# Taking the feed-forward part's low operand halves off GpSimd and onto VectorE, with VectorE's step reordered

## The chip, the core and the metric

One core of one Trainium2 chip runs the whole kernel in one launch. The metric is device time in microseconds (us), the median over several runs. Engines are named as the profile names them: PE (TensorE's matmuls), PEld (its weight loads), DVE (VectorE), ACT (ScalarE), POOL (GpSimd), SP (SyncE, which here issues DMAs).

## What is computed

One encoder layer over 2048 tokens of width 1024. The change lies in its last part, the feed-forward block:

```
x = x + (gelu(gate) * val) @ w_down,   [gate | val] = dwconv3(rmsnorm(x) @ w_up),   D_FF = 2816
out = rmsnorm(x)
```

`w_up` is 1024 x 5632, `w_down` 2816 x 1024, the convolution is depthwise over three neighbouring tokens, everything is float32. Attention, the recurrent group and the output projection come before and are not touched.

## The kernel before, in words

**Split operands.** Each float32 matrix operand is split in two: a high part (`hi`, the operand rounded to fp32r) and a low part (`lo` = operand minus `hi`). A product is three matmuls, hi by hi, hi by lo and lo by hi. ACT makes the high part with a copy, and another engine makes the low part with one subtraction (`tensor_tensor`, subtract), which needs the high part. In the feed-forward block POOL makes the low parts of the weights and of some activations, DVE the others.

**Class `Up`** computes rmsnorm(x) @ w_up. It runs 44 steps: 22 channel blocks for the first half of the tokens (steps 0 to 21), then the same 22 for the second half (steps 22 to 43). A step multiplies a 2 x 2 block of weights with a 2 x 2 block of activations by seven products instead of eight (`product(s, 0)` to `product(s, 6)`), on sums and differences of the blocks. A product is 12 matmuls of 128 x 128 by 128 x 512, a step 84. Its seven activation operands ("11", "T2", "T3", "21", "T1", "22", "T4" in `ORDER`) live in 15 slots `b0` to `b14` of 128 x 2048 values, and stay for 22 steps. In step 21 they are exchanged (`refill`, `refill_more`): the second half's blocks are fetched from `h2_d` (`fetch`, tile `b..f`), differences formed (`minus`, L773), and each is split again (`high_b`, L789 on ACT; `low_b`, L795).

Each step's weights come by DMA into `wr` (`load_w`, L809); DVE forms four sums (`sums_w`, L817 to L820, tile `sw`); ACT and POOL split four groups g = 0 to 3 into tiles `wg` (`high_w`, L832; `low_w`, L837). Groups 0, 1, 2 have 128 x 1024 values, group 3 has 128 x 512. Group 0 serves products 0 and 3, group 1 products 1 and 2, group 2 products 4 and 5, group 3 product 6.

The products land in eight PSUM banks `q`. DVE (`add`, L876; `c21`, L928) and ACT (copies, L886 and L913) join them to the rows `u` of gate and value. ACT then starts the convolution (`center`, L946: middle tap and bias), DVE adds the outer two taps (`taps`, L954, one `scalar_tensor_tensor` each), ACT applies GeLU (`gelu`, L960), DVE multiplies gate and value (`glu`, L966) and SP stores the result to `a_d`. The value's half of a step's convolution is done in the next step.

**Class `Down`** computes the product with `w_down` in 48 pieces of 48 matmuls or fewer. `load_w` and `load_a` fetch, `split_w` and `split_a` split (both L74 for the high and L77 for the low part; weights in slots `b`, activations in `dah`, `dal`). It begins inside step 43, by `prefetch`.

**Order.** PE, DVE, ACT and POOL run `Up` and `Down` in the order in which the code is written, each engine its own instructions in turn. SP's DMAs, and the few `Up` instructions issued while the output projection runs (`first_weights`), are ordered by the scheduler. An instruction that waits holds up everything behind it on its engine.

## Time and profile before

| | us |
|---|---|
| median of 3 runs (2776.57 to 2779.14) | 2779.02 |
| the profiled execution, its own time | 2781.06 |
| span of that execution in the trace | 2779.3 |
| PE busy in the span | 2649.6 (95%) |
| DVE busy | 1929.2 (69%) |
| ACT busy | 1291.5 (46%) |
| POOL busy | 1090.6 (39%) |

`Up` runs on PE from about 1329 to 2277 us of the span, `Down` from there to the end. The span is 1.8 us shorter than the profiled execution's own time, and that execution is 2.0 us above the median. How to read it: busy PE is not the whole answer, since a matmul at half clock is also busy; so stretches are compared by their length, by what PE waits for in them, and by the granted clock.

### The profile page before, as it was taken

Reading aid. Unit: us, or ns where it says so; the run is one execution under the profiler, and the core shown is the slowest. Engines: PE = TensorE matmul, PEld = TensorE weight load, DVE = VectorE, ACT = ScalarE, POOL = GpSimd, SP = SyncE. Lnnn points to the kernel's source line nnn. Section 1 sums busy time; section 2 is a strip of 40 time slices with the busy share of each in tenths; the row PEclk is TensorE's granted clock in tenths of the full one; section 3 lists DMA queues with packets and bytes.
Section 4 is the critical chain, followed back from the end, with each engine's and each line's share of the span. In section 5 each row is a group of like instructions: output and inputs, shape, how many; then the busy total and the mean of one; then the engine's idle time right before and its main releaser. Section 6 shows DMA issues by size and latency. Waiting matters only on the chain.

```text
span 2779.3 us, 33388 instructions
## 1 busy us (share of the span) xinstructions
PE 2649.6 (95%) x13168; PEld 2147.5 (77%) x13168; DVE 1929.2 (69%) x2055; ACT 1291.5 (46%) x1625; POOL 1090.6 (39%) x628
## 2 busy tenths in 40 slices
PE   7999999899999999999799999879999999999998
PEld 6878778678888887778577777657777778888887
DVE  5453554699999998443699999999999983222333
ACT  4343453588888888322443433343343351122222
POOL 1013322256676767300454554545455553012000
PEclk9999999899999999999899999989999999999999
DMA  5422121401111012334222122312222244344443
GB/s 191 118 84 70 63 85 67 184 18 54 54 54 54 24 31 72 125 125 163 91 84 76 69 83 76 114 61 84 76 81 72 76 168 165 127 154 174 159 159 129
DMA packets 122381, 271.90 MB, mean 98 GB/s; under 512 B 15792, under 2 KB 52144, under 8 KB 115056
## 3 DMA queue, kind: packets, MB, share of 16 engines
q1 hardware_dynamic: 120016, 263.63, 27.7%
q0 software_dynamic: 1632, 4.46, 0.5%
q8 instruction: 103, 1.69, 0.3%
q10 hardware_dynamic: 576, 1.69, 0.2%
q14 instruction: 54, 0.44, 0.1%
HBM read 187.94 MB, written 81.79 MB: 97 GB/s over the span
## 4 chain that ended last, share of the span: by engine, by line
PE 59%; DVE 25%; issue 9%; ACT 4%; POOL 2%; DMA 1%; SPq 0%; DVEq 0%; ACTq 0%; POOLq 0%
DVE acc L954 11%; PE sc L407 7%; PE pd L82 6%; PE pd L80 6%; PE pd L81 6%; PE ps L82 4%; PE ps L81 4%; PE ps L80 4%; PE tp L433 4%; DVE u L876 4%; PE q L864 2%; PE po L82 2%; PE po L81 2%; PE po L80 2%; PE pv L465 2%
## 5 line engine op out<-in xcount | busy, mean ns | idle before, releaser
L954 DVE SCALAR_TENSOR_TENSOR acc<-u,prm,acc 128x1023 f32<-128x1023 f32 (+1 forms) x176 | 474.7, 2697 | 66.9 <-ACT acc L946 63.8
L837 POOL TENSOR_TENSOR wg<-sw,wg 128x1024 fp32r<-128x1024 f32 x88 | 260.8, 2964 | 328.4 <-ACT wg L832 328.4
L77 DVE TENSOR_TENSOR dal<-dal,dah 128x2048 fp32r<-128x2048 f32 (+1 forms) x47 | 111.4, 2374 | 292.7 <-ACT dah L74 292.6
L946 ACT ACTIVATE acc<-u,prm 128x1023 f32<-128x1023 f32 (+1 forms) x88 | 109.3, 1242 | 334.9 <-DVE u L876 196.2
L416 ACT ACTIVATE e<-e,mn 128x2048 f32<-128x2048 f32 x128 | 256.2, 2007 | 15.9 <-DVE mn L411 15.9
L837 POOL TENSOR_TENSOR wg<-wr,wg 128x1024 fp32r<-128x1024 f32 x88 | 204.2, 2321 | 119.0 <-ACT wg L832 119.0
L407 PE MATMUL sc<-ks,qt 64*128 64x512 f32 x1536 | 234.5, 421 | 16.1 <-DVE mn L411 11.9
L74 ACT ACTIVATE dah<-dal 128x2048 fp32r<-128x2048 f32 (+1 forms) x47 | 83.1, 1769 | 309.0 <-DMA dal<-a_d 293.0
L90 POOL TENSOR_TENSOR r<-ss,mhalf 128x1 f32<-128x1 f32 x48 | 27.5, 574 | 482.0 <-DVE ss L88 477.2
L427 DVE SCALAR_TENSOR_TENSOR e<-e,rc,e 128x1024 f32<-128x1024 f32 x128 | 213.9, 1672 | 2.3
L82 PE MATMUL ps<-hT_hi,wl 128*128 128x512 f32 x512 | 199.6, 390 | 0.0
L81 PE MATMUL ps<-hT_lo,wh 128*128 128x512 f32 x512 | 199.6, 390 | 0.0
L80 PE MATMUL ps<-hT_hi,wh 128*128 128x512 f32 x512 | 199.5, 390 | 0.0
L407 PEld LDWEIGHTS sc<-ks,qt 64*128 64x128 f32 x1536 | 147.9, 190 | 62.1 <-DVE mn L411 20.4
L77 POOL TENSOR_TENSOR wTl<-wf,wTh 128x512 fp32r<-128x512 f32 x64 | 127.4, 1991 | 112.4 <-ACT wTh L74 109.8
L411 DVE CUSTOM_DVE_ANT_0 e<-sc,strip,mn 128x1024 f32<-128x1024 f32 x128 | 159.1, 1280 | 16.6 <-PE sc L407 13.8
L876 DVE TENSOR_TENSOR u<-q,u 128x512 f32<-128x512 f32 x220 | 150.6, 685 | 12.8 <-PE q L864 6.9
L77 POOL TENSOR_TENSOR wTl<-wg,wTh 128x1024 fp32r<-128x1024 f32 x64 | 158.1, 2470 | 0.0
L411 DVE CUSTOM_DVE_ANT_0 e<-sc,strip 128x1024 f32<-128x1024 f32 x128 | 150.8, 1212 | 9.0 <-PE sc L407 6.4
L433 PEld LDWEIGHTS tp<-ident,e 128*128 128x128 f32 x1024 | 111.8, 142 | 46.2 <-ACT wTh L74 19.8
L433 PE MATMUL tp<-ident,e 128*128 128x128 f32 x1024 | 142.2, 283 | 0.0
L77 POOL TENSOR_TENSOR wl<-ws,wh 128x1024 fp32r<-128x1024 f32 x16 | 39.1, 2447 | 223.9 <-DVE wh L76 212.0
(348 smaller groups left out, 7122.0 us busy)
## 6 DMA issues: line engine op xcount, KB each, us to landing
wr<-in_w_up_dram SPq DMA_DIRECT2D x88, 512.0 KB, 4.2
dal<-a_d SPq DMA_DIRECT2D x39, 1024.0 KB, 5.0
a_d<-acc SPq DMA_DIRECT2D x66, 256.0 KB, 2.0
xt<-in_x_dram SPq DMA_DIRECT2D x30, 512.0 KB, 4.7
ws<-in_w_qkr_dram SPq DMA_DIRECT2D x16, 512.0 KB, 3.4
qt<-q_d SPq DMA_DIRECT2D x32, 256.0 KB, 3.3
ks<-k_d SPq DMA_DIRECT2D x8, 1024.0 KB, 7.8
vt<-v_d SPq DMA_DIRECT2D x8, 1024.0 KB, 7.1
```

The costliest lines, as they stand in the source:

```text
L77: lo_eng.tensor_tensor(out=lo, in0=src, in1=hi, op=ALU.subtract)
L80: T.matmul(ps, lh, rh, start=first, stop=False)
L81: T.matmul(ps, lh, rl, start=False, stop=False)
L82: T.matmul(ps, ll, rh, start=False, stop=last)
L407: T.matmul(self.sc[c][:, n * CH:(n + 1) * CH], l[rows, q], r[rows, kk], start=i == 0, stop=i == 2)
L411: V.tensor_tensor_reduce(out=self.e[c][:, hf * 1024:(hf + 1) * 1024], in0=self.sc[c], in1=strip[:, off:off + 1024], scale=SLOPES[self.h], ...
L416: A.activation(out=self.e[c], in_=self.e[c], func=AF.Exp, scale=-1.0, bias=self.mn[:, 2 * c + 1:2 * c + 2], accum_out=self.s[c])
L427: V.scalar_tensor_tensor(out=e0, in0=e1, scalar=self.rc, in1=e0, op0=ALU.mult, op1=ALU.add)
L433: T.transpose(tp[:, m, :], self.e[0][:, (4 * i + m) * P:(4 * i + m + 1) * P], ident)
L837: G.tensor_tensor(out=t[:, 1], in0=src, in1=t[:, 0], op=ALU.subtract)
L876: V.tensor_tensor(out=out, in0=a, in1=b_, op=ALU.add)
L954: V.scalar_tensor_tensor(out=acc[:, 0:n], in0=u[:, o + tap:o + tap + n], scalar=prm[:, C_FW + 3 * m + tap:C_FW + 3 * m + tap + 1], in1=acc ...
```

## The change

Every low part of `Up` and `Down` that POOL made is now made on DVE: `low_w` (all weight groups), the splits of "11", "21" and "22", and every `split_w`. After it, POOL is left with one 128 x 1 power per row tile there. Inside `step` some calls move: group 3's low part from the step's start to behind `sums_w`; group 0's to behind `glu`, beside group 1's; group 2's high part to before `center(s, 0)`; and ACT's copy of bank "a" to behind `center(old, 1)` and `gelu(old)`.

```diff
--- before.py
+++ after.py
@@ -834,7 +834,7 @@
 
         def low_w(self, s, g):
             t, src = self.w[s][g]
-            G.tensor_tensor(out=t[:, 1], in0=src, in1=t[:, 0], op=ALU.subtract)
+            V.tensor_tensor(out=t[:, 1], in0=src, in1=t[:, 0], op=ALU.subtract)
 
         def first_weights(self):
             self.load_w(0)
@@ -882,16 +882,16 @@
                 self.c21(old)
             if s > 0:
                 self.high_w(s, 3)
-                self.low_w(s, 3)
-            A.activation(out=ug[:, Y], in_=q("a"), func=AF.Copy)
             if old is not None:
                 self.center(old, 1)
                 self.gelu(old)
+            A.activation(out=ug[:, Y], in_=q("a"), func=AF.Copy)
             if more:
                 self.load_w(s + 1)
                 self.high_w(s + 1, 0)
-                self.low_w(s + 1, 0)
                 self.sums_w(s + 1)
+            if s > 0:
+                self.low_w(s, 3)
             self.product(s, 1)
             hook(1)
             add(uv[:, X], q("d"), ug[:, Y])
@@ -902,9 +902,11 @@
             add(uv[:, X], q("b"), uv[:, X])
             if more:
                 self.high_w(s + 1, 1)
-                self.low_w(s + 1, 1)
             if old is not None:
                 self.glu(old)
+            if more:
+                self.low_w(s + 1, 0)
+                self.low_w(s + 1, 1)
             self.product(s, 3)
             hook(3)
             self.product(s, 4)
@@ -915,9 +917,10 @@
             self.product(s, 5)
             add(ug[:, Y], q("e"), ug[:, Y])
             hook(5)
+            if more:
+                self.high_w(s + 1, 2)
             self.center(s, 0)
             if more:
-                self.high_w(s + 1, 2)
                 self.low_w(s + 1, 2)
             self.taps(s, 0)
             self.product(s, 6)
@@ -999,7 +1002,7 @@
                 raw["21"] = self.fetch(0, 1)
             elif i == 4:
                 raw["T1"] = self.minus(raw["12"], raw["11"])
-                self.split_b("11", G)
+                self.split_b("11", V)
             elif i == 5:
                 raw["T2"] = self.minus(raw["22"], raw["T1"])
                 self.high_b("T2")
@@ -1011,25 +1014,25 @@
                 self.split_b("T3", V)
                 raw["T4"] = self.minus(raw["21"], t2)
                 self.sl.give(t2)
-                self.split_b("21", G)
+                self.split_b("21", V)
 
         def refill_more(self, i):
             if i == 0:
                 self.split_b("T1", V)
-                self.split_b("22", G)
+                self.split_b("22", V)
             elif i == 3:
                 self.split_b("T4", V)
 
         def run(self, down):
             self.low_b("T2", V)
             self.split_b("T3", V)
-            self.split_b("21", G)
+            self.split_b("21", V)
             self.high_w(0, 2)
             self.low_w(0, 2)
             self.split_b("T1", V)
             self.high_w(0, 3)
             self.low_w(0, 3)
-            self.split_b("22", G)
+            self.split_b("22", V)
             self.split_b("T4", V)
             hooks = {NFF - 1: self.refill, NFF: self.refill_more, self.STEPS - 1: lambda i: (self.done_b(i), down.prefetch(i))}
             for s in range(self.STEPS):
@@ -1085,7 +1088,7 @@
             elif i == 2:
                 self.load_w(0, 1)
             elif i == 4:
-                self.split_w(0, 0, G)
+                self.split_w(0, 0, V)
             elif i == 5:
                 self.split_a(0, V)
 
@@ -1120,7 +1123,7 @@
                 nc.sync.dma_start(out[t * P:(t + 1) * P, :], y)
 
             self.load_a(1)
-            self.split_w(0, 1, G)
+            self.split_w(0, 1, V)
             self.split_a(1, V)
             nc.sync.dma_start(g_b, g_fin.partition_broadcast(P))
             last = len(self.order) - NG
@@ -1130,7 +1133,7 @@
                 if i + 2 < len(self.order):
                     self.load_a(i + 2)
                 if c == 0 and n == 0 and g + 2 < NG:
-                    self.split_w(0, g + 2, G)
+                    self.split_w(0, g + 2, V)
                 if i + 2 < len(self.order):
                     self.split_a(i + 2, V)
                 if g == 0:
@@ -1151,7 +1154,7 @@
                 if n == 0 and c == NCH - 1:
                     self.sl.give(*self.w.pop((0, g)))
                     self.load_w(1, g)
-                    self.split_w(1, g, G)
+                    self.split_w(1, g, V)
 
     phase1()
     kp_stack = ExitStack()
```

In the listings below the changed kernel's line numbers are two or three higher from L886 on (L954 of before is L957 there). `u` with a number is a row buffer, `q` with a number a PSUM bank.

**DVE, one step of the second half.** From the last add into the gate row of a step to the middle of the next step: before,

```order
L876 TENSOR_TENSOR u_11979<-q_15558,u_11979 128x512
L954 SCALAR_TENSOR_TENSOR acc<-u_11979,prm,acc 128x1025 x2
L928 TENSOR_TENSOR u_11980<-q_15580,u_11980 128x512
L817 TENSOR_TENSOR sw<-wr 128x512
L818 TENSOR_TENSOR sw<-wr 128x512
L819 TENSOR_TENSOR sw<-sw,wr 128x512
L820 TENSOR_TENSOR sw<-wr,sw 128x512
L876 TENSOR_TENSOR u_11982<-q_15626,u_11981 128x512
L954 SCALAR_TENSOR_TENSOR acc<-u_11980,prm,acc 128x1025 x2
L876 TENSOR_TENSOR u_11982<-q_15642,u_11982 128x512
L966 TENSOR_TENSOR acc<-acc 128x1025
L876 TENSOR_TENSOR u_11981<-q_15626,u_11981 128x512
```

and the same place in the changed kernel up to the new low part of group 3,

```order
L876 TENSOR_TENSOR u_11979<-q_15558,u_11979 128x512
L837 TENSOR_TENSOR wg_15572<-sw,wg_15572 128x1024
L957 SCALAR_TENSOR_TENSOR acc<-u_11979,prm,acc 128x1025 x2
L931 TENSOR_TENSOR u_11980<-q_15580,u_11980 128x512
L817 TENSOR_TENSOR sw<-wr 128x512
L818 TENSOR_TENSOR sw<-wr 128x512
L819 TENSOR_TENSOR sw<-sw,wr 128x512
L820 TENSOR_TENSOR sw<-wr,sw 128x512
L837 TENSOR_TENSOR wg_15607<-wr,wg_15607 128x512
```

A low part of group 2 now stands between the add and the gate's taps, and one of group 3 behind the four sums. The next rows of the changed kernel:

```order
L876 TENSOR_TENSOR u_11982<-q_15625,u_11981 128x512
L957 SCALAR_TENSOR_TENSOR acc<-u_11980,prm,acc 128x1025 x2
L876 TENSOR_TENSOR u_11982<-q_15641,u_11982 128x512
L969 TENSOR_TENSOR acc<-acc 128x1025
L837 TENSOR_TENSOR wg_15617<-wr,wg_15617 128x1024
L837 TENSOR_TENSOR wg_15655<-sw,wg_15655 128x1024
L876 TENSOR_TENSOR u_11981<-q_15625,u_11981 128x512
L876 TENSOR_TENSOR u_11982<-q_15641,u_11981 128x512
L876 TENSOR_TENSOR u_11981<-q_15690,u_11981 128x512
```

Two low parts, of groups 0 and 1, now stand between the product of gate and value and the three adds.

**ACT, the same place.** From the end of one step's products to the GeLU in the next: before,

```order
L940 ACTIVATE u_11979<-halo 128x2
L946 ACTIVATE acc<-u_11979,prm 128x1025
L832 ACTIVATE wg_15047<-sw 128x1024
L832 ACTIVATE wg_15079<-wr 128x512
L886 ACTIVATE u_11981<-q_15065 128x512
L940 ACTIVATE u_11980<-halo 128x2
L946 ACTIVATE acc<-u_11980,prm 128x1025
L960 ACTIVATE acc<-acc 128x1025
```

and in the changed kernel,

```order
L832 ACTIVATE wg_15044<-sw 128x1024
L943 ACTIVATE u_11979<-halo 128x2
L949 ACTIVATE acc<-u_11979,prm 128x1025
L832 ACTIVATE wg_15079<-wr 128x512
L943 ACTIVATE u_11980<-halo 128x2
L949 ACTIVATE acc<-u_11980,prm 128x1025
L963 ACTIVATE acc<-acc 128x1025
L888 ACTIVATE u_11981<-q_15065 128x512
```

The high part of group 2 (`wg<-sw`) moved ahead of `center`, and the copy of bank "a" (`u_11981<-q`) behind the GeLU.

**SP, around the exchange of operands in step 21.** `b8f` is block "11" of the second half, `b2f` is "12", `wr` are weights: before,

```order
L969 DMA a_d_111<-acc 128x511
L809 DMA wr<-in_w_up_dram 128x1024
L986 DMA b8f<-h_d_102 128x4x128
L986 DMA b8f<-h_d_103 128x4x128
L986 DMA b8f<-h_d_104 128x4x128
L986 DMA b8f<-h_d_105 128x4x128
L986 DMA b2f<-h_d_106 128x4x128
L986 DMA b2f<-h_d_107 128x4x128
```

and in the changed kernel,

```order
L972 DMA a_d_111<-acc 128x511
L989 DMA b2f<-h_d_106 128x4x128
L989 DMA b8f<-h_d_102 128x4x128
L989 DMA b8f<-h_d_103 128x4x128
L989 DMA b8f<-h_d_104 128x4x128
L989 DMA b8f<-h_d_105 128x4x128
L989 DMA b2f<-h_d_107 128x4x128
L989 DMA b2f<-h_d_108 128x4x128
```

The half load of `wr` that stood ahead of the eight fetches of "11" and "12" now comes after them (and after those of "21").

## Rows read from the trace of the kernel before

**Rows 1.** The page: busy time of each engine (share of the span, instructions), and the chain that ended last by engine.

```profile
PE 2649.6 (95%) x13168; PEld 2147.5 (77%) x13168; DVE 1929.2 (69%) x2055; ACT 1291.5 (46%) x1625; POOL 1090.6 (39%) x628
...
PE 59%; DVE 25%; issue 9%; ACT 4%; POOL 2%; DMA 1%; SPq 0%; DVEq 0%; ACTq 0%; POOLq 0%
```

**Rows 2.** Busy time by stretch: from:to and length in us, busy us of PE, PEld, DVE, ACT, POOL (instructions), PE's granted clock, DMA share, GB/s. The inner boundaries are the first matmuls of `Up` steps 1, 2, 21, 22, 23 and of `Down`.

```profile
1327.00:1365.93 38.93, 22.89 (x80) 17.75 (x81) 19.78 (x23) 16.38 (x15) 19.68 (x6) 0.74 0.32 107
1365.93:1385.32 19.39, 19.39 (x86) 15.79 (x84) 18.18 (x15) 8.72 (x12) 10.52 (x4) 1.00 0.24 82
1385.32:1772.91 387.59, 372.75 (x1597) 298.55 (x1596) 357.35 (x283) 150.38 (x208) 199.82 (x76) 1.00 0.22 76
1772.91:1793.45 20.54, 19.63 (x85) 15.70 (x84) 18.89 (x16) 9.87 (x12) 11.88 (x5) 1.00 0.61 173
1793.45:1847.84 54.39, 29.89 (x86) 21.56 (x85) 50.32 (x26) 19.55 (x19) 22.98 (x7) 0.69 0.20 67
1847.84:2276.61 428.77, 412.73 (x1765) 329.92 (x1764) 393.34 (x312) 169.83 (x233) 220.25 (x83) 1.00 0.23 81
2276.61:2300.00 23.39, 19.32 (x70) 14.63 (x69) 21.18 (x10) 14.92 (x9) 14.76 (x3) 0.85 0.94 343
2300.00:2779.30 479.30, 470.76 (x2044) 383.20 (x2042) 140.80 (x109) 106.95 (x83) 49.76 (x25) 0.99 0.43 151
```

**Rows 3.** What PE waited for, from 1385.32 to 1772.91 (steps 2 to 20) and from 1847.84 to 2276.61 (steps 23 to 43): us in total, times, longest; in each stretch the only row.

```profile
PE q L864 <- DVE u L876: 14.8, 17, 0.9
...
PE q L864 <- DVE u L876: 16.0, 18, 0.9
```

**Rows 4.** The timeline of DVE in a step of the first half: start, us, engine, line, instruction, count [idle before <- who ended it].

```profile
1600.05 6.50 DVE L954 SCALAR_TENSOR_TENSOR acc<-u,prm,acc 128x1023 f32<-128x1023 f32 x2
...
1608.20 2.20 DVE L876 TENSOR_TENSOR u<-q,u 128x512 f32<-128x512 f32 x3
...
1611.81 4.63 DVE L954 SCALAR_TENSOR_TENSOR acc<-u,prm,acc 128x1023 f32<-128x1023 f32 x2 [1.41 <-ACT acc L946]
...
1616.96 1.18 DVE L817 TENSOR_TENSOR sw<-wr 128x512 f32<-128x512 f32 x1
...
1618.06 0.68 DVE L818 TENSOR_TENSOR sw<-wr 128x512 f32<-128x512 f32 x1
```

**Rows 5.** The timeline of POOL in the same step.

```profile
1599.75 2.38 POOL L837 TENSOR_TENSOR wg<-wr,wg 128x1024 fp32r<-128x1024 f32 x1 [2.70 <-ACT wg L832]
...
1602.09 3.37 POOL L837 TENSOR_TENSOR wg<-sw,wg 128x1024 fp32r<-128x1024 f32 x1
```

**Rows 6.** The timeline of DVE at three places with POOL idle.

```profile
1327.22 2.29 DVE L795 TENSOR_TENSOR b9r<-b5f,b0r 128x2048 fp32r<-128x2048 f32 x1
...
2266.98 2.61 DVE L954 SCALAR_TENSOR_TENSOR acc<-u,prm,acc 128x1025 f32<-128x1025 f32 x2 [0.77 <-ACT acc L946]
...
2285.16 1.23 DVE L966 TENSOR_TENSOR acc<-acc 128x1025 f32<-128x1025 f32 x1
```

**Rows 7.** The timeline of PE, POOL and DVE in step 0.

```profile
1342.62 0.80 PE L864 MATMUL q<-b12r,wg 128*128 128x512 f32 x1 [6.10 <-ACT u L886]
...
1343.54 4.55 POOL L795 TENSOR_TENSOR b1r<-b3f,b6r 128x2048 fp32r<-128x2048 f32 x1
...
1348.12 4.41 DVE L795 TENSOR_TENSOR b3r<-b7f,b4r 128x2048 fp32r<-128x2048 f32 x1 [8.00 <-POOL b1r L795]
...
1355.72 0.80 PE L864 MATMUL q<-b14r,wg 128*128 128x512 f32 x1 [8.44 <-DVE u L876]
```

**Rows 8.** The timeline of POOL, SP, DVE and PE around the exchange (steps 21 and 22).

```profile
1779.69 2.28 POOL L837 TENSOR_TENSOR wg<-wr,wg 128x512 fp32r<-128x512 f32 x1
...
1782.00 0.33 SPq L809 DMA_DIRECT2D wr<-in_w_up_dram  x1
...
1782.39 2.08 SPq L986 DMA_DIRECT2D b8f<-h_d  x4
...
1794.44 5.28 DVE L773 TENSOR_TENSOR b9f<-b2f,b8f 128x2048 f32<-128x2048 f32 x1
...
1814.74 0.79 PE L864 MATMUL q<-b5r,wg 128*128 128x512 f32 x1 [9.43 <-DVE b5r L795]
...
1816.81 6.67 DVE L773 TENSOR_TENSOR b1f<-b0f,b12f 128x2048 f32<-128x2048 f32 x1
...
1826.54 0.50 PE L864 MATMUL q<-b4r,wg 128*128 128x512 f32 x1 [3.56 <-ACT u L886]
...
1836.56 0.80 PE L864 MATMUL q<-b2r,wg 128*128 128x512 f32 x1 [5.40 <-DVE u L876]
```

**Rows 9.** The timeline of DVE and PE at the start of `Down`.

```profile
2287.06 19.14 DVE L77 TENSOR_TENSOR dal<-dal,dah 128x2048 fp32r<-128x2048 f32 x3 [0.67 <-ACT dah L74]
...
2290.90 0.50 PE L81 MATMUL pd<-b4r,dah 128*128 128x512 f32 x1 [1.65 <-POOL b4r L77]
...
2293.05 0.80 PE L82 MATMUL pd<-b6r,dal 128*128 128x512 f32 x1 [1.65 <-DVE dal L77]
```

**Rows 10.** Groups by form: instructions, us in total, mean ns of one | idle before.

```profile
L832 ACT ACTIVATE wg<-sw 128x1024 fp32r<-128x1024 f32 x88 | 91.8, 1043 | 16.6 <-DVE sw L819 16.6
...
L946 ACT ACTIVATE acc<-u,prm 128x1025 f32<-128x1025 f32 x44 | 54.9, 1248 | 269.8 <-DVE u L876 196.2 <-issue 73.5
...
L913 ACT ACTIVATE u<-q 128x512 f32<-128x512 f32 x44 | 25.5, 580 | 4.5 <-PE q L864 4.5
```

## The prediction

> **What bounds the kernel now.** I read the page first. PE is busy for 95% of the span, yet a quarter of the chain that ended last is DVE [rows 1], so in places PE waits for DVE. The table by stretch says where [rows 2]. Between steps 1 and 2 of `Up` PE is busy for the whole 19.39 us: this is a step's floor, 84 matmuls with no wait. The 19 steps after it take 387.59 us, 20.40 each, the 21 steps of the second half 428.77 us, 20.42 each, all at full clock. Three stretches are worse: step 0 with what stands ahead of it (38.93 us, clock 0.74), step 22 (54.39 us, clock 0.69), and the first 23.39 us of `Down` (clock 0.85). These five make up nearly all that PE loses after 1327 us; in the last 479.30 us it is busy for 470.76.
>
> In the even stretches PE waits for one thing, a DVE add, 0.9 us in most steps [rows 3]: product 4 goes on in the bank that the add has to read first. DVE is late because it is full: 357.35 busy us of 387.59, 92% [rows 2]. And why it is full stands in the timelines. One pair of taps takes 6.50 us, the other 4.63 [rows 4], while a pair with POOL idle takes 2.61 [rows 6]. The 6.50 can be followed: POOL runs from 1599.75 to 1602.13 and from 1602.09 to 1605.46 [rows 5]; the first tap, issued at 1600.05, can only end 1.3 us after 1602.1, the second 1.1 us or so after 1605.46, at 1606.55. Each waits for POOL's instruction to end and then runs its own 1.3 us. POOL in turn is stretched to 3.37. So the taps pay 6.50 + 4.63 - 2 x 2.61 = 5.9 us a step for low parts that POOL makes, and the first of the four sums pays 0.5 (1.18 against 0.68) [rows 4].
>
> **The change, part by part.**
>
> *DVE's load in a step.* Gone: 5.9 + 0.5 = 6.4 us. Added: three low parts of 128 x 1024 at 1.23 (as the 128 x 1025 on two SBUF operands [rows 6]) and one of 128 x 512 at 0.68 [rows 4], 4.4 us. DVE's sum: four sums 2.7, six adds 4.1 (0.68 each), taps 5.2, the product of gate and value 1.2, low parts 4.4, together 17.6 us, against PE's 19.39. DVE no longer sets the pace, if its order puts no wait on PE.
>
> *The order.* I count from the end of product 5. ACT: high part of group 2, 1.04, then `center`, 1.25 [rows 10]. DVE in that time: the add 0.7, then the low part of group 2 from 1.1 to 2.3, then taps to 5.0, `c21` to 5.7. ACT: `center` of the value to 6.9, GeLU to 8.0, and only now the copy of bank "a", 0.6, to 8.6. PE has meanwhile run product 6 and products 0 to 2, four times 2.77, and wants that bank at 11.1: 2.5 us to spare. DVE goes on: sums to 8.4, low part of group 3 to 9.1, the add that PE waits for today to 9.8; PE wants it at 13.8. The new wait, DVE for ACT's high part of group 2, lies where DVE waits today for `center` (1.41 us between the adds' end at 1610.40 and 1611.81 [rows 4]) and holds up the taps, `c21` and all that follows, which is in this count. The low parts of groups 0 and 1, moved behind `glu`, are due in the next step, that of group 3 at product 6: all with over 5 us to spare. Weights: `wr` is released when group 3's low part is done, a few us later in the step, and the load is needed a step later; SP issues it in the same place. So I cost the order at nothing; the cover is that 2.5 us on ACT, and beyond it each us of delay costs 1 us a step.
>
> *Even steps.* Before, 19 + 1 + 21 steps and the floor step took 19.39 + 387.59 + 20.54 + 428.77 = 856.3 us [rows 2]; now 42 x 19.39 = 814.4. **Gain 41.9.** It cannot be more; below, a wait of 0.6 us left in each step would leave 17.
>
> *Step 0.* PE waits 6.10 us for ACT and 8.44 for the add behind DVE's 4.41 us low part of "T4", which began only when POOL's 4.55 us low part of "22" had ended at 1348.09 [rows 7]. Now DVE makes all of them in turn, 2.2 each from 1331.2 on: "T3", "21", group 2, "T1", group 3, "22", "T4", to about 1344.1; sums to 1346.6, the first add to 1347.3 in place of 1355.7. PE's rest follows as before, so **gain 8.4**; ends are 0 and 14.5, both waits.
>
> *Step 22.* Before, 54.39 us: two waits of 9.43 and 5.40 on DVE among others, DVE instructions of 128 x 2048 at 5.28 and 6.67 in place of 2.29 [rows 6, 8]. The fetch of "11" stood in SP's queue behind a `wr` load that waited for POOL's low part of group 3 (ended 1781.97, load issued 1782.00, fetch 1782.39 [rows 8]); in the new order of SP it can go when product 0 of step 21 is done, some 6 us sooner. DVE can then form "T1" as soon as two adds on product 4 are done, 3.9 us ahead of the boundary of steps 21 and 22 (product 4 ends two products, 5.5, ahead of it). From there, at 2.3 a piece: T1, low of "11", an add 0.7, T2; ACT's high part of T2 1.9 and of group 2 1.04; low part of group 2 1.2, taps 2.6, T3, low of T2. That is 18.9, ready 15.0 after the boundary, where PE would want it at 5.5: the long wait stays. Then five more pieces of 2.3 (two of them POOL's today), `c21` 0.7, `center`, GeLU and the copy 2.9: PE's product 3 starts 30.1 after the boundary, behind the moved copy; four products make 41.2, and half clock after that wait some 2. So 43.2, **gain 11.2**. Ends: 0, and 24, if the long waits of rows 8 went.
>
> *`Down`.* Three low parts took 19.14 us on DVE against three of POOL's, and PE waited 1.65 for each side and then ran at half clock [rows 9]; of the stretch 4.1 us are idle on PE, and clock 0.85 takes some 2.9 of the 19.32 busy: 7 us to win [rows 2]. Alone, the six low parts take 14 us and the first two are ready before or 1 to 2 us after PE wants them: **gain 4.5**, ends 0 and 7. Further on, eight more of at most 2.29 lie on a DVE busy for 140.80 of 479.30 us [rows 2]: nothing. The two low parts under the output projection: 2.5 us, beside PE: nothing; at worst 2.5.
>
> **Sum:** 41.9 + 8.4 + 11.2 + 4.5 = 66.0 us. The profiled execution's 2781.06 becomes 2715.1; it stands 2.0 above the median, so I forecast 2779.0 - 66.0 = **2713.0**.
>
> **A rule against it.** DVE is at 92% [rows 2], and its taps are long beside POOL, short without it [rows 4, 6]. The Trainium skill, Perfetto Trace Analysis, section Optimizing Scalar/DVE Operations, says that where VectorE is saturated, moving work off it, even to GpSimd, may make sense, and adds that the two share a read port, "so offloading operations between those two might not help". Its first half speaks against moving work onto an engine at 92%, its second half for it. By the first half the sum would be the first rival's; by the rows it is the 66.0 above. The trace is with the second half so far, by the 6.50 against 2.61.
>
> **Rivals.**
>
> *DVE's time is its own (slower).* If the taps are long for a reason that stays (their operands, ACT or PE beside them), DVE keeps its 18.89 busy us of a step [rows 2] and gets 4.4 more: 23.3, and 42 steps cost 2.9 more each, 122 us: 2901. It decides once DVE's work in a step passes 20.4, 2.8 above my 17.6. For it: 92% busy. Against it: three pairs of taps without POOL run in 2.6 like [rows 6]. Chance 0.03. The first half of the skill's rule would end there.
>
> *Only the even steps gain.* The long waits in steps 0 and 22 and at `Down` move to other work on DVE, which now does all splits in turn: 2779.0 - 41.9 = 2737. For it: the long wait in step 22 is DVE's already. Against: pieces of 2.3 for 4.4 to 6.7. Chance 0.08.
>
> *A wait stays in each step.* The 2.5 us of cover fail, by longer handovers between engines than I count, and 0.6 us a step remain: 2779 - 17 - 24 = 2738. Chance 0.05.
>
> *No change:* PE's wait goes elsewhere whole. Chance 0.03.
>
> **Chances and range.** The forecast has 0.81; its own range, with the terms at the likelier parts of their bounds (5 to 11, 39 to 42, 3 to 20, 1 to 6), is 2700 to 2731. To 2735 for the nearest rivals. Faster by over 0.2% (5.6 us, about what a measurement can tell): 0.81 + 0.08 + 0.05 = 0.94; same 0.03; slower 0.03.
>
> **What would show it.** Right: no PE wait on an add in the even steps, 19.4 us a step, clock 1.0; taps 1.3 us each, DVE near 17 us a step with pauses; step 22 near 43 us with a wait of some 9 us for T2's low part and one for ACT's copy of bank "a". Wrong: steps over 19.6, taps over 1.5, or a step 22 over 50.

## The result, and the profile after

The changed kernel takes 2708.99 us (median of four runs, 2706.97 to 2711.47) against 2778.44 for the kernel before (median of four): a ratio of 0.9751, with a 95% interval of 0.9735 to 0.9768. The forecast was 2713.0, with a range of 2700 to 2735. The profiled execution of the changed kernel took 2708.57 us, its span is 2706.6.

The page of the changed kernel, busy time by engine and the chain that ended last, answers to [rows 1]:

```profile
PE 2629.2 (97%) x13168; PEld 2143.8 (79%) x13168; DVE 1841.4 (68%) x2248; ACT 1306.4 (48%) x1625; POOL 543.5 (20%) x435
...
PE 88%; DVE 4%; issue 2%; ACT 2%; POOL 2%; DMA 1%; SPq 0%; POOLq 0%; DVEq 0%; ACTq 0%
```

DVE runs 193 instructions more and is busy 88 us less: POOL's busy time was not added to DVE's. DVE's part of the chain fell from 25% to 4%.

The table by stretch of the changed kernel answers to [rows 2]; the columns are the same, the boundaries are the matmul with which product 1 of step 0 goes on (its first matmul with a low part, after PE's last break), the first matmuls of steps 1, 2, 21, 22, 23 and of `Down`, and a point 23.39 us later:

```profile
1325.23:1351.50 26.27, 21.04 (x72) 16.09 (x72) 22.49 (x20) 15.68 (x14) 0.00 (x0) 0.81 0.38 128
1351.50:1370.89 19.39, 19.39 (x85) 15.78 (x84) 16.59 (x20) 9.70 (x12) 0.00 (x0) 1.00 0.23 82
1370.89:1739.37 368.48, 368.48 (x1598) 299.80 (x1597) 316.38 (x362) 157.64 (x209) 0.00 (x0) 1.00 0.23 82
1739.37:1758.76 19.39, 19.39 (x86) 15.77 (x84) 18.43 (x19) 7.82 (x9) 0.00 (x0) 1.00 0.82 244
1758.76:1801.48 42.72, 24.48 (x86) 18.48 (x84) 38.88 (x32) 21.48 (x20) 0.00 (x0) 0.76 0.17 60
1801.48:2209.43 407.95, 407.95 (x1766) 331.24 (x1764) 347.30 (x394) 176.94 (x230) 0.00 (x0) 1.00 0.24 85
2209.43:2232.82 23.39, 21.56 (x93) 16.96 (x92) 21.85 (x14) 15.21 (x11) 0.00 (x0) 1.00 0.99 363
2232.82:2706.60 473.78, 465.59 (x2022) 378.94 (x2020) 149.70 (x116) 106.98 (x83) 8.79 (x16) 0.99 0.43 151
```

In the even steps PE is busy in every microsecond: 368.48 of 368.48, 407.95 of 407.95. The difference of the two profiled spans, 72.7 us (the medians differ by 69.5), splits like this (before and after, us):

| stretch | before | after | difference | forecast |
|---|---|---|---|---|
| up to that matmul of product 1 of step 0 | 1329.56 | 1325.23 | -4.3 | 0 |
| from there to step 1 | 36.37 | 26.27 | -10.1 | -8.4 |
| steps 1 to 21 | 427.52 | 407.26 | -20.3 | with the next: -41.9 |
| steps 23 to 43 | 428.77 | 407.95 | -20.8 | |
| step 22 | 54.39 | 42.72 | -11.7 | -11.2 |
| `Down` to the end | 502.69 | 497.17 | -5.5 | -4.5 |

Of the 4.3 us ahead of `Up`, 3.4 are there already when the output projection begins (1101.68 us before, 1098.27 after), in stages that the change does not touch; in the traces of the fourteen kernels of this study that moment lies between 1097.7 and 1101.9 whatever the edit.

PE's waits in steps 0 and 22 of the changed kernel answer to [rows 7, 8]; the timeline of PE, in brackets the idle time and who ended it:

```profile
1337.21 0.80 PE L864 MATMUL q<-b12r,wg 128*128 128x512 f32 x1 [4.81 <-ACT u L888]
1343.12 0.51 PE L864 MATMUL q<-b14r,wg 128*128 128x512 f32 x1 [0.42 <-DVE u L876]
...
1764.10 0.50 PE L864 MATMUL q<-b13r,wg 128*128 128x512 f32 x1 [1.90 <-ACT b13r L789]
1773.31 0.80 PE L864 MATMUL q<-b5r,wg 128*128 128x512 f32 x1 [8.72 <-DVE b5r L795]
1787.62 0.79 PE L864 MATMUL q<-b4r,wg 128*128 128x512 f32 x1 [7.42 <-ACT u L888]
...
2223.36 0.50 PE L82 MATMUL pd<-b6r,dal 128*128 128x512 f32 x1 [1.36 <-DVE dal L77]
```

Step 0's second wait is gone (8.44 to 0.42), step 22 keeps the long wait for the low part of "T2" and then waits for the moved copy of bank "a", and `Down` keeps one wait of 1.36 of its two of 1.65 [rows 9].

DVE's timeline in one steady step of the changed kernel answers to [rows 4]:

```profile
1602.23 1.23 DVE L837 TENSOR_TENSOR wg<-sw,wg 128x1024 fp32r<-128x1024 f32 x1 [0.45 <-ACT wg L832]
1603.46 2.60 DVE L957 SCALAR_TENSOR_TENSOR acc<-u,prm,acc 128x1023 f32<-128x1023 f32 x2
...
1606.59 0.68 DVE L817 TENSOR_TENSOR sw<-wr 128x512 f32<-128x512 f32 x1
...
1610.32 2.60 DVE L957 SCALAR_TENSOR_TENSOR acc<-u,prm,acc 128x1023 f32<-128x1023 f32 x2
...
1613.43 1.22 DVE L969 TENSOR_TENSOR acc<-acc 128x1023 f32<-128x1023 f32 x1
...
1617.73 1.42 DVE L876 TENSOR_TENSOR u<-q,u 128x512 f32<-128x512 f32 x2 [0.82 <-PE q L864]
1620.48 0.69 DVE L876 TENSOR_TENSOR u<-q,u 128x512 f32<-128x512 f32 x1 [1.33 <-PE q L864]
```

Both pairs of taps take 2.60 us, where they took 6.50 and 4.63, and now DVE waits for PE (0.82 and 1.33 us a step).

### The profile page after: what moved, and what is told of

It is laid out like the page before. It is cut to its first block, busy times and chain, and to the rows that moved or that the text cites. A ratio compares the mean times of both kernels' runs of the same rounds, so it can differ in the third digit from the quotient of the medians.

```text
span 2706.6 us, 33137 instructions
## 1 busy us (share of the span) xinstructions
PE 2629.2 (97%) x13168; PEld 2143.8 (79%) x13168; DVE 1841.4 (68%) x2248; ACT 1306.4 (48%) x1625; POOL 543.5 (20%) x435
## 4 chain that ended last, share of the span: by engine, by line
PE 88%; DVE 4%; issue 2%; ACT 2%; POOL 2%; DMA 1%; SPq 0%; POOLq 0%; DVEq 0%; ACTq 0%
PE q L864 30%; PE sc L407 7%; PE pd L82 6%; PE pd L80 6%; PE pd L81 6%; PE ps L82 5%; PE ps L81 5%; PE ps L80 4%; PE tp L433 4%; PE po L82 2%; PE po L81 2%; PE po L80 2%; PE pv L465 2%; PE pv L81 2%; PE pv L80 2%
## 5 line engine op out<-in xcount | busy, mean ns | idle before, releaser
L77 DVE TENSOR_TENSOR dal<-dal,dah 128x2048 fp32r<-128x2048 f32 (+1 forms) x47 | 99.2, 2110 | 274.5 <-ACT dah L74 274.5
L957 DVE SCALAR_TENSOR_TENSOR acc<-u,prm,acc 128x1023 f32<-128x1023 f32 (+1 forms) x176 | 226.0, 1284 | 7.6 <-ACT acc L949 1.4
L832 ACT ACTIVATE wg<-sw 128x1024 fp32r<-128x1024 f32 x88 | 93.4, 1061 | 285.2 <-PE q L864 281.5
L864 PE MATMUL q<-b4r,wg 128*128 128x512 f32 x352 | 117.5, 395 | 7.4 <-ACT u L888 7.4
L864 PE MATMUL q<-b12r,wg 128*128 128x512 f32 x352 | 119.7, 401 | 4.8 <-ACT u L888 4.8
```

The costliest lines, as they stand in the source:

```text
L77: lo_eng.tensor_tensor(out=lo, in0=src, in1=hi, op=ALU.subtract)
L864: T.matmul(ps, l, r[:, k, :], start=new is not None and k == 0 and n == 0, stop=k == 3 and n == 2, skip_group_check=True)
L957: V.scalar_tensor_tensor(out=acc[:, 0:n], in0=u[:, o + tap:o + tap + n], scalar=prm[:, C_FW + 3 * m + tap:C_FW + 3 * m + tap + 1], in1=acc ...
```

## The experiments

All ratios are to the kernel before, on the same chip, with 95% intervals. My theory when they were planned: POOL's low parts make DVE late (the taps wait for POOL), so taking them off POOL is what brings the even steps to their floor, and the new order is only what lets DVE carry them. The rival: the order alone does it.

**Run e1: the engine without the order.** The kernel before, with every `G` of the diff turned into `V` and no line moved.

```diff
-            G.tensor_tensor(out=t[:, 1], in0=src, in1=t[:, 0], op=ALU.subtract)
+            V.tensor_tensor(out=t[:, 1], in0=src, in1=t[:, 0], op=ALU.subtract)
...
-                self.split_b("11", G)
+                self.split_b("11", V)
```

> All low parts on VectorE, but in the order of the kernel before. My theory (both halves of the change are needed): the taps run in 1.3 us each, but VectorE stands at group 0's low part until ScalarE has done center, GeLU and the high part, some 3 us a step, so a step takes about 21.8 us, step 22 about 48, and the whole 2815 us (2790 to 2840), slower than before. Rival A (the engine move alone is the gain, the order a trimming): steps of 19.4 to 19.8 and 2709 to 2725. Rival B (the order is the gain, GpSimd was harmless): as before, 2779.

Measured: 2828.43 us, ratio 1.0178 (1.0161 to 1.0195): slower than before by 50 us. Steps alternate between 20.84 and 23.3 us. DVE's timeline in this run:

```profile
1599.84 1.23 DVE L837 TENSOR_TENSOR wg<-sw,wg 128x1024 fp32r<-128x1024 f32 x1 [2.35 <-ACT wg L832]
1600.98 2.60 DVE L954 SCALAR_TENSOR_TENSOR acc<-u,prm,acc 128x1023 f32<-128x1023 f32 x2
...
1607.39 1.23 DVE L837 TENSOR_TENSOR wg<-wr,wg 128x1024 fp32r<-128x1024 f32 x1 [2.61 <-ACT wg L832]
```

The taps are short at once (2.60 a pair), so what stretched them was POOL. And DVE is not full: busy 224.35 of 300 us (1400 to 1700), 75%. It is late because it stands still: twice a step a low part waits for ACT's high part, 69.4 us in those 300, and the sums and adds that PE needs are queued behind it.

**Run e2: the order without the engine.** The changed kernel with every low part given back to POOL, so the four moves of the diff alone.

```diff
             if s > 0:
                 self.high_w(s, 3)
-                self.low_w(s, 3)
-            A.activation(out=ug[:, Y], in_=q("a"), func=AF.Copy)
             if old is not None:
                 self.center(old, 1)
                 self.gelu(old)
+            A.activation(out=ug[:, Y], in_=q("a"), func=AF.Copy)
...
```

> The new order, with all low parts on GpSimd as before. My theory: taps beside GpSimd stay stretched, 4 to 6.5 us a pair where they meet it; steps between 19.4 and 20.5 us, step 0, step 22 and the start of Down near the times of before; 2740 to 2775 us. Rival A: 2779, nothing gained. Rival B: 2709 to 2715.

Measured: 2736.82 us, ratio 0.9845 (0.9831 to 0.986). This is the main miss of the study (e6 is another): I had the order alone too slow. Its even steps take 19.39 and 19.43 us. The row of 1400 to 1700 us, in the columns of the table above:

```profile
1400.00:1700.00 300.00, 300.00 (x1301) 244.29 (x1301) 270.55 (x232) 126.29 (x170) 173.19 (x63) 1.00 0.23 81
```

PE is busy 300 of 300 with POOL busy 173.19. So of the 69 us, 42 need no change of engine. Instruction by instruction, DVE and POOL have the same order here as in the kernel before; what differs in a step is two moves on ACT.

**Runs h1 and h2: one ACT move each, in the kernel before.** h1 moves the copy of bank "a", h2 the high part of group 2.

```diff
h1:
-            A.activation(out=ug[:, Y], in_=q("a"), func=AF.Copy)
             if old is not None:
                 self.center(old, 1)
                 self.gelu(old)
+            A.activation(out=ug[:, Y], in_=q("a"), func=AF.Copy)
h2:
+            if more:
+                self.high_w(s + 1, 2)
             self.center(s, 0)
             if more:
-                self.high_w(s + 1, 2)
                 self.low_w(s + 1, 2)
```

> The kernel before with one edit: ACT's copy of bank "a" stands behind the center of the value and GeLU; all low parts stay where they were, on POOL too. The run with the changed kernel's order alone took 2736.82 us, and its DVE and POOL have the order of before; so it differs from before by two moves on ACT, and this is one of them. Theory A (the high part of group 2 is the move that counts, because POOL then makes its low part while DVE waits for center): here the taps stay long, the steps stay at 20.2 to 20.4 us, time 2767 (2755 to 2779). Theory B (the copy is the move that counts, because center and GeLU come 0.6 us sooner and the second taps start ahead of POOL's low part of group 0): steps at 19.4 us, time near 2737.

> The kernel before with the other edit alone: ACT makes the high part of group 2 ahead of the center of the gate. Theory A: POOL's low part of group 2 runs while DVE waits for center, the first taps of a step fall from 6.50 to about 4 us, the first sum from 1.18 to 0.68, PE's wait of 0.9 us on the add goes, steps at 19.4 us, time 2740 (2735 to 2752). Theory B: it gives nothing by itself, steps at 20.4, time 2779.

Measured: h1 2771.70 us, ratio 0.9971 (0.9962 to 0.998); h2 2736.54, ratio 0.985 (0.9833 to 0.9867). The high part of group 2, moved ahead of `center` (h2), does by itself all that the whole order does with POOL at work, and the moved copy of bank "a" (h1) brings 8 us: theory A. One row of the kernel before that was not shown (DVE, the product of gate and value), for the sum below:

```profile
1607.07 1.21 DVE L966 TENSOR_TENSOR acc<-acc 128x1023 f32<-128x1023 f32 x1
```

DVE's timeline in h1, and POOL's:

```profile
1610.15 4.61 DVE L954 SCALAR_TENSOR_TENSOR acc<-u,prm,acc 128x1023 f32<-128x1023 f32 x2 [1.41 <-ACT acc L946]
...
1615.29 1.19 DVE L817 TENSOR_TENSOR sw<-wr 128x512 f32<-128x512 f32 x1
...
1618.92 4.61 DVE L954 SCALAR_TENSOR_TENSOR acc<-u,prm,acc 128x1023 f32<-128x1023 f32 x2
1623.45 0.68 DVE L876 TENSOR_TENSOR u<-q,u 128x512 f32<-128x512 f32 x1
1624.05 2.81 DVE L966 TENSOR_TENSOR acc<-acc 128x1023 f32<-128x1023 f32 x1
```

```profile
1619.10 3.35 POOL L837 TENSOR_TENSOR wg<-wr,wg 128x1024 fp32r<-128x1024 f32 x1 [3.17 <-ACT wg L832]
1622.41 3.38 POOL L837 TENSOR_TENSOR wg<-sw,wg 128x1024 fp32r<-128x1024 f32 x1
```

DVE's timeline in h2, and POOL's:

```profile
1598.09 4.26 DVE L955 SCALAR_TENSOR_TENSOR acc<-u,prm,acc 128x1023 f32<-128x1023 f32 x2 [1.41 <-ACT acc L947]
...
1602.87 0.68 DVE L817 TENSOR_TENSOR sw<-wr 128x512 f32<-128x512 f32 x1
...
1605.99 4.62 DVE L955 SCALAR_TENSOR_TENSOR acc<-u,prm,acc 128x1023 f32<-128x1023 f32 x2
...
1611.13 2.82 DVE L967 TENSOR_TENSOR acc<-acc 128x1023 f32<-128x1023 f32 x1
```

```profile
1596.63 2.41 POOL L837 TENSOR_TENSOR wg<-sw,wg 128x1024 fp32r<-128x1024 f32 x1 [3.15 <-ACT wg L832]
1598.99 2.27 POOL L837 TENSOR_TENSOR wg<-wr,wg 128x512 fp32r<-128x512 f32 x1
```

These rows bear on the length of a step. In each kernel add up what POOL can stretch on DVE: two pairs of taps, the first sum, the product of gate and value. Before: 4.63 + 6.50 + 1.18 + 1.21 = 13.52. h1: 4.61 + 4.61 + 1.19 + 2.81 = 13.22, 0.30 less, and its steps are 0.29 shorter (20.26 for 20.55). h2: 4.26 + 4.62 + 0.68 + 2.82 = 12.38, 1.14 less, and its steps are 1.16 shorter (19.39). In the kernel before and in h1 DVE's row sets the step. In h2 PE sets it (busy 300 of 300), so there the sum only says that DVE's row fits; e2, where it is 3.96 + 4.61 + 0.68 + 2.82 = 12.07, has the same steps. In h2 POOL's low part of group 2 starts at 1596.63, while DVE runs its adds and waits 1.41 us for `center`; in the kernel before it starts 1.0 us after the first tap, so the second tap waits for it, group 3's low part for that tap, and the first sum for that low part. In these steps the kernel before lacked 1.15 us of DVE to be at PE's floor, and this move supplies at least that.

**Run g1: group 0's low part ahead of the sums again**, in the changed kernel.

```diff
                 self.high_w(s + 1, 0)
+                self.low_w(s + 1, 0)
                 self.sums_w(s + 1)
...
-                self.low_w(s + 1, 0)
                 self.low_w(s + 1, 1)
```

> The changed kernel with one of its moves undone: group 0's low part stands ahead of the four sums again, behind ScalarE's center and GeLU. My theory: this is the move that counts; VectorE waits there about 2 to 3 us a step, a step takes 20.8 us, step 22 about 48, the whole 2775 us (2755 to 2790). Rival A (order is a trimming): 2709 to 2720.

Measured: 2775.51 us, ratio 0.9985 (0.9975 to 0.9994); 20.76 us a step. The row of DVE's timeline:

```profile
1613.20 1.23 DVE L837 TENSOR_TENSOR wg<-wr,wg 128x1024 fp32r<-128x1024 f32 x1 [3.68 <-ACT wg L832]
```

This one line takes back 66 of the 69 us. The high part that it waits for stands on ACT behind `center`, which waits for DVE's `c21`, then GeLU and the copy; DVE stands still for 3.68 us and PE waits for the add behind it, 48.3 us in 43 waits.

**Run g3: the high part of group 2 behind `center` again**, in the changed kernel: the move of h2 undone where DVE makes the low part.

```diff
-            if more:
-                self.high_w(s + 1, 2)
             self.center(s, 0)
             if more:
+                self.high_w(s + 1, 2)
                 self.low_w(s + 1, 2)
```

> The changed kernel with the high part of group 2 put back behind the center of the gate, so that DVE's low part of group 2 starts about 1.2 us later, and with it the taps, the add c21, center, GeLU and the copy of bank a. With all low parts on DVE this move was covered, by the prediction: the copy is done 2.5 to 2.8 us before PE wants it. Theory: still 19.4 us a step, time 2709 (2706 to 2712). Rival: what counted in the kernel before (this one move alone brought 2736.54 from 2780.06 us there) counts here too, and each step gets 0.5 to 1.2 us longer: 2730 to 2760.

Measured: 2712.10 us, ratio 0.9752 (0.9736 to 0.9768): no change against the changed kernel's 0.9751. DVE's waits in this run, 1400 to 1700 us:

```profile
DVE wg L837 <- ACT wg L832: 35.3, 15, 2.4
DVE u L876 <- PE q L864: 7.0, 16, 0.4
```

DVE waits 2.4 us a step for ACT where the changed kernel's waits 0.45, and pays with its own spare: its wait for PE falls from 34.4 us to 7.0. The steps stay at 19.4; 0.8 us more go in each of steps 1 and 22, 0.5 in step 23. The same line is worth 44 us where POOL makes the low parts; where DVE does, the traces show 2 to 3 us, which the medians do not tell from nothing.

**Run e6: the low parts on DVE, and POOL makes each once more** (896 of every 1024 values, 512 of group 3), into a bf16 buffer that nothing reads, in all steps from 1 on.

```diff
+            if s > 0:
+                n = 4 if g == 3 else 7
+                G.tensor_tensor(out=self.scr[:, 0:n], in0=src[:, 0:n], in1=t[:, 0, 0:n], op=ALU.subtract)
```

> The changed kernel, and GpSimd makes each step's low parts once more (896 of 1024 values, 512 for group 3) into a scratch tile in bf16 that nobody reads: the work beside VectorE is back, no wait on it but the release of the weight tiles. My theory: the taps are stretched again to 4 to 6.5 us a pair, VectorE has over 22 us of work a step and becomes the bound: 22 to 23.5 us a step, 2820 to 2890 us. Rival B (GpSimd beside VectorE is harmless; the taps were long for their own reasons): 2709 to 2715.

Measured: 2786.75 us, ratio 1.0023 (1.0011 to 1.0035): 78 us above the changed kernel. DVE's timeline in this run:

```profile
1599.13 4.34 DVE L961 SCALAR_TENSOR_TENSOR acc<-u,prm,acc 128x1023 f32<-128x1023 f32 x2
...
1612.33 3.52 DVE L961 SCALAR_TENSOR_TENSOR acc<-u,prm,acc 128x1023 f32<-128x1023 f32 x2 [0.27 <-ACT acc L953]
```

DVE's pairs of taps are long again, 4.34 and 3.52 us, and it is busy 292.3 of 300 us. The direction is as expected, the size was set too high (the time lies below the expected range): by these rows DVE waits only where the two engines' instructions meet, not for the sum of POOL's work.

**Run e8: POOL writes and reads nothing.**

```diff
+            if 1 <= s <= 8:
+                for _ in range(12):
+                    G.memset(self.scr, 0.0)
```

> The changed kernel, and in steps 1 to 8 POOL fills a buffer of 128 x 896 bf16 twelve times a step with zeros: it writes, and reads nothing. If DVE and POOL take turns only where both read two operands, the taps in these steps stay at 1.3 us each and the time is within 3 us of 2709. If any access of POOL takes the turn, the taps there go to 2 us or more, DVE falls behind, and the eight steps are longer than 19.4 us.

Measured: 2709.28 us (a single execution). POOL did not follow the steps: it ran the 96 fills in one piece, from 1321.2 to 1407.8, so it lies beside the taps of three steps alone. The end of it on POOL's timeline, and DVE beside it:

```profile
1347.33 60.42 POOL L931 MEMSET scr<- 128x896 bf16 x67
```

```profile
1351.54 2.60 DVE L961 SCALAR_TENSOR_TENSOR acc<-u,prm,acc 128x1023 f32<-128x1023 f32 x2
...
1362.63 1.22 DVE L973 TENSOR_TENSOR acc<-acc 128x1023 f32<-128x1023 f32 x1
```

Beside an unbroken row of POOL writes the taps take 2.60 a pair and the product 1.22, as with POOL idle, and a fill takes 844 to 847 ns throughout. With e6, where POOL writes the same buffer and also reads, this says that what is shared is reading.

**Run e3: the large splits on POOL again**, in the changed kernel: "11", "21", "22" and every `split_w`; the weight groups' low parts stay on DVE.

```diff
-                self.split_b("11", V)
+                self.split_b("11", G)
...
-                self.split_w(0, 0, V)
+                self.split_w(0, 0, G)
...
```

> The changed kernel with the splits of blocks 11, 21 and 22 and every split_w given back to POOL; the low parts of the weight groups in the steps stay on DVE. What the engine move brings beyond the new order (2736.82 to 2708.99 us) lies by my reading in step 0, step 22 and the start of the Down part, in the 128 x 2048 and 128 x 1024 pieces that POOL makes there. Then the even steps stay at 19.4 us, step 22 comes to about 50 us instead of 42.6, step 0 near the 42 us of the order-only run, and the time is about 2730 (2720 to 2738). Rival: the weight groups' low parts in steps 0, 1, 22 and 23 are what counts there; then step 22 stays near 43 and the time near 2711.

Measured: 2720.99 us, ratio 0.9795 (0.9775 to 0.9816). The time is just inside the expected range, the place is not as expected. By the boundaries of the table above step 22 takes 54.39 us before, 51.55 in e2, 45.78 here and 42.72 in the changed kernel. So of the 8.8 us by which step 22 is longer in e2 than in the changed kernel, the weight groups bring 5.8, and the splits 3.1, most of it PE's wait for the low part of "T4":

```profile
1808.24 0.50 PE L864 MATMUL q<-b7r,wg 128*128 128x512 f32 x1 [2.42 <-DVE b7r L795]
```

The rest of what the splits bring is 5.6 us between the first matmuls of products 1 and 6 of step 0 (33.93 against 28.30) and 2.5 in `Down`. The weight groups' part does not come by earlier fetches: in e2 no engine waits for a fetch from 1756 to 1828 us, and DVE forms "T1" right behind the adds, with no idle time before it:

```profile
1774.01 5.34 DVE L773 TENSOR_TENSOR b9f<-b2f,b8f 128x2048 f32<-128x2048 f32 x1
```

"T1" starts 1.9 us ahead of the boundary in e2, behind a pair of taps of 4.61 us and a product of gate and value of 2.82; in e3, where these take 2.6 and 1.22, it starts 3.9 us ahead.

**Run e5: the copy of bank "a" back ahead of `center`**, in the changed kernel.

```diff
+            A.activation(out=ug[:, Y], in_=q("a"), func=AF.Copy)
             if old is not None:
                 self.center(old, 1)
                 self.gelu(old)
-            A.activation(out=ug[:, Y], in_=q("a"), func=AF.Copy)
```

> The changed kernel with ACT's copy of bank a put back ahead of the center of the value and GeLU. In the even steps the copy is done 2.8 us ahead of PE, so there nothing changes: 19.4 us a step. In step 22 PE's wait of 7.42 us for this copy goes, but the add on bank d, which product 4 needs, still comes at 1787.92 us in DVE's order and the low part of T4 at 1795.03 to 1797.31: PE's product 6 there can start 1.3 us sooner than now and not more. Step 22 at 41 to 42 us, time 2707.5 (2705 to 2710). Rival: the copy's wait is the price of step 22, and 4 to 7 us come back: 2703.

Measured: 2707.46 us, ratio 0.9733 (0.9718 to 0.9748), not to be told from the changed kernel. PE's timeline in step 22:

```profile
1790.26 0.50 PE L864 MATMUL q<-b2r,wg 128*128 128x512 f32 x1 [4.33 <-DVE u L876]
1798.97 0.50 PE L864 MATMUL q<-b7r,wg 128*128 128x512 f32 x1 [1.10 <-DVE b7r L795]
```

The wait of 7.42 us is gone, one of 4.33 for the add and one of 1.10 for "T4" stand in its place; steps 22 and 23 together are 1.4 us shorter (60.65 for 62.08, here and below between first matmuls of product 6). DVE's chain is the limit there, and the copy was only its last link.

**Runs e7 and e9: that chain in another order.** A hook is a place between two products at which the code of the exchange runs. e7 forms T2 and T3 one hook earlier, makes the low parts of T2 and T3 one behind the other, then T4 and "21", and puts the split of T1 behind `c21`. e9 also moves the split of T4 ahead of the product of gate and value.

```diff
e7:
-            hook(0)
             if old is not None:
                 self.c21(old)
+            hook(0)
...
+                raw["T2"] = self.minus(raw["22"], raw["T1"])
+                self.high_b("T2")
+                raw["T3"] = self.minus(raw["22"], raw["12"])
...
e9, on top:
             add(uv[:, X], q("b"), uv[:, X])
+            if s == NFF:
+                self.split_b("T4", V)
...
-            elif i == 3:
-                self.split_b("T4", V)
```

> The changed kernel with the exchange of operands in steps 21 and 22 put in another order on DVE: the differences T2 and T3 are formed one hook earlier, the low parts of T2 and T3 stand one behind the other, the difference T4 and the split of 21 come after, the split of T1 stands behind c21 and that of 22 one hook later. If step 22's 42.7 us is DVE's chain to the low part of T2 (wait of 8.72 us) and then the chain to the copy of bank a (7.42 us), this shortens step 22 to 38 to 40 us and the time to 2705 (2702 to 2708). Rival: the fetches or ACT's high parts set the waits; then step 22 stays at 42 to 43 and the time at 2709. A third way: a later low part (21 or 22) comes too late, and step 22 grows to 45 or more, 2712.

> The kernel with the reordered exchange (run e7, 2703.96 us) with one more move in step 22: the split of T4 stands behind the add on bank b, ahead of the product of gate and value and of two low parts. In e7 PE waited 2.71 us for T4's low part, made from 1791.19 us, behind those three pieces of 1.22, and ran at half clock after that wait; step 23 took 24.0 us. Theory: the low part of T4 is then done 3.7 us sooner, ahead of PE, step 23 takes 19.4 to 20 us, and the time is 2699.5 (2697 to 2703). Rival: the two low parts of weights, now 2.2 us later, or the adds behind them hold PE in step 23 instead; then step 23 stays over 22 and the time at 2704.

Measured: e7 2703.96 us, ratio 0.973 (0.9709 to 0.975), not to be told from the changed kernel by these intervals; e9 2702.32, ratio 0.9719 (0.9704 to 0.9733), the fastest kernel of the study, its interval just clear of the changed kernel's. By the traces, steps 22 and 23 take 62.08 us in the changed kernel, 59.37 in e7 (35.37 + 24.00) and 56.37 in e9 (35.38 + 20.99). The e9 expectation of 2699.5 was 3 us too low: step 23 did not come to 19.4. PE's timeline in e9:

```profile
1766.27 0.79 PE L864 MATMUL q<-b8r,wg 128*128 128x512 f32 x1 [2.56 <-DVE b8r L795]
1779.82 0.79 PE L864 MATMUL q<-b1r,wg 128*128 128x512 f32 x1 [6.56 <-ACT u L888]
1785.50 0.50 PE L864 MATMUL q<-b4r,wg 128*128 128x512 f32 x1 [1.15 <-DVE u L876]
1803.67 0.50 PE L864 MATMUL q<-b1r,wg 128*128 128x512 f32 x1 [1.28 <-ACT u L888]
```

The wait of 8.72 us for the low part of "T2" has become 2.56, e7's wait of 2.71 for "T4" is gone, the wait for the copy is still 6.56, and a new one of 1.28 for the copy comes in step 23.

## Why the prediction was right, and where its reasons were not

*Even steps (41.9 forecast, 41.1 measured).* The size is right, since PE's floor sets it; the 0.8 us that it lacks are the floor of the second half, 407.95 us in 21 steps, 19.43 each and not 19.39. The chain of reasons is right for the changed kernel: taps 1284 ns on average (226.0 us in 176), no PE wait on an add, DVE with pauses. But the step "so I cost the order at nothing" fails as a statement of who brings what. The forecast put the whole gain down to the 6.4 us that DVE gets back from POOL. DVE lacked only 1.15 us a step, and ACT's high part of group 2, moved ahead of `center`, supplies that with POOL still at work (h2, 2736.54 us). The engine alone costs 50 us (e1), and one low part in the old place takes back nearly all the gain (g1). The four corners are 2778 (neither), 2737 (order), 2828 (engine), 2709 (both). The number came out because the forecast costed the two together, in one timeline from the end of product 5; it could not have said which half to keep.

*The cover of 2.5 us on ACT.* Right: in the steady step the copy of bank "a" ends at 1609.38; product 3, which writes that bank next, ends at 1614.9 and takes 2.77 us, so it starts 2.8 us behind the copy. g3 uses up 1.9 us of DVE's spare without a longer step.

*The cause of the long taps.* Right: e1 and e6 switch them off and on. The point not seen is that turns depend on who starts first. In [rows 4, 5] POOL starts 0.30 us ahead of the tap: each tap waits for one POOL instruction, 6.50 us the pair, and the product of gate and value behind them takes 1.21. In h1 the tap starts 0.18 us ahead of POOL: the pair takes 4.61, and the product waits, 2.81. So a shift of half a microsecond on ACT moves the price from one instruction to another.

*The rule against it.* The Trainium skill, Perfetto Trace Analysis, section Optimizing Scalar/DVE Operations, was weighed with both its halves. For the changed kernel the trace is with the second half: DVE is busy 88 us less with more to do. In e1 the result is on the side of the first half, but not for its reason, since DVE was 75% busy there.

*Step 0 (8.4 forecast, 10.1 measured).* The low part of "T4" ends at 1339.93 and the first add starts at 1342.38. In the time of the trace of before, which is 4.33 us later here, that is 1344.3 and 1346.7; the forecast had 1344.1 and 1346.6 (sums done). The 1.7 us above the forecast are the wait for ACT, 4.81 for 6.10, and the smaller part at half clock (0.81 granted for 0.72 from the same matmul to step 1).

*Step 22 (43.2 forecast, 42.72 measured).* DVE forms "T1" from 1754.82, 3.94 us ahead of the boundary (3.9 forecast); the fetch of "11" is issued 5.2 us sooner against that boundary than before (some 6 forecast). The low part of "T2" releases PE 14.55 us after the boundary (15.0 forecast), product 3 starts 28.86 after it (30.1 forecast), behind the moved copy as said; it and the three products after it take 13.9 us where 13.1 were counted, so the sum is closer than its parts. The term was a count of DVE's pieces in order, and the order of the instructions gave it.

*`Down` (4.5 forecast, 5.5 measured).* One of the two waits is left, 1.36 us, within the 1 to 2 us that were said. e3 puts 2.5 of it on the splits of the weights.

*Elsewhere.* The 4.3 us ahead of `Up` were not forecast and are mostly not the change's (above). Under the output projection 0.6 us less, not more: from its start to the first `Up` matmul the changed kernel takes 145.62 us, the one before 146.25.

*The rivals.* "DVE's time is its own" fell with the taps at 1.28 us. "Only the even steps gain" describes, by accident, the order-only run: 2736.82 against its 2737.

## What to carry to other kernels

When two engines read the same memory in turns, an engine that looks full (92% busy) may be full of waiting: compare the same instruction with and without its neighbour before believing the share. Before moving work to another engine, ask by how much the late engine is late; here it was 1.15 us a step, and starting POOL's low part of group 2 some 2.5 us earlier against DVE's adds, in a pause of DVE, was enough (2.4 us behind their end before, at their end in h2). And when work does move onto an engine that runs in order, place each piece behind the instruction that the bottleneck waits for, not where its own input happens to be ordered: the same move is worth +50 or -70 us by that alone.

## What the runs showed of the hardware

*Turns by whole instructions.* h1's rows can be followed to 0.1 us: the first tap from 1618.92 to 1620.2; POOL's low part, issued at 1619.10, ends at 1622.45, 2.25 after the tap; the second tap ends at 1623.53, 1.1 after that; POOL's next low part, issued at 1622.41, ends at 1625.79, 2.26 after the tap; the product, issued at 1624.05, ends at 1626.86, 1.1 after POOL. Once it is its turn, each takes no longer than it does alone (a tap 1.28, a low part 2.38 where POOL starts first [rows 5]). The Trainium skill, SBUF — State Buffer, section SBUF: two separate sides, says the same: the shared pair is an exclusive lock, and whichever starts first has it for the whole instruction. These rows agree.

*Only reads, and only two of them.* The add at 1623.45 in h1 (one operand in PSUM, `q`, one in SBUF, `u`) takes 0.68 us, as elsewhere, while POOL's second low part, with two operands to read, has its turn (from 1623.53). Writes by POOL cost the taps nothing (e8, one execution). The Trainium skill, SBUF — State Buffer, section Who interferes with whom, says that a DVE instruction with two SBUF inputs contends with a GpSimd instruction that reads SBUF and not with one that only writes it; e6, where POOL reads, and e8, where it only writes, agree.

*An engine's busy time counts its turns.* DVE's busy time in 300 us was 275.32 before, 224.35 in e1 (on fewer steps), 256.24 in the changed kernel at full speed, and 273.68 in h2, which is as fast in these steps. Busy shares of two engines that take turns do not rank kernels.
